# A down projection in two phases, with its weight sums made in DRAM: an encoder layer on one Trainium2 core

## The chip, the cores and the metric

The kernel runs on one core of a Trainium2 chip. TensorE (PE) multiplies, VectorE (DVE), ScalarE (ACT) and GpSimd (POOL) work on the elements, SyncE (SP) issues most of the transfers, and POOL issues some of its own. The metric is the device time of one execution in microseconds; less is better.

## The reference

One layer of a streaming encoder, for a prompt of 1024 frames and a sample of 32 frames, in float32. Both groups lie side by side as T = 1056 token columns.

```python
h = rms_norm(x); z = h @ w_in              # split into qa ka va | qb fb ib ob | ga gb
ya = sliding_window_attention(qa, ka, va)  # 16 query heads, 2 kv heads, sink logits, bias
yb = hgrn2(qb, fb, ib, ob)                 # gated recurrence, 8 heads
x = x + rms_norm((sig(ga) * (ya @ w_br_a) + sig(gb) * (yb @ w_br_b)) @ w_out)
a, u = split(rms_norm(x) @ w_up)           # two halves of 2816
a = causal_conv3(a)
x = x + rms_norm((gelu(a) * u) @ w_down)   # w_down is 2816 x 1024
y = x + (p @ w_ple) * sig(x @ w_ple_gate)
```

## The kernel before

Activations lie with features on the 128 partitions and tokens along the row. Every float32 factor is split into a rounded high part and a low part (ACT makes the high part by a cast, DVE the low part by a subtraction), and a product is three matmuls: high by high, high by low, low by high.

The stages run one after another: norm and attention (to about 330 us), the recurrence, branch mix and output projection, the up projection with the convolution (units of L2060 to L2140), the down projection (L2188 to L2270), and the gate of the last line of the reference.

The **up and down projections** use a block scheme with seven products instead of eight: the weight is cut in 2 x 2 blocks, the activations too, and sums of blocks are multiplied. For the weight of the down projection with blocks a11, a12, a21, a22, the seven left factors are: 0: a11, 1: a11+a21+a22, 2: a12, 3: a11+a21, 4: a21+a22, 5: a22, 6: a12 + factor 1. The right factors (sums of activation blocks) are written to DRAM by the up projection, in `s_d` and `a_d`, and loaded again as operands `dop`.

The down projection runs over three parts of the 2816 rows (`KP`, 3, 4 and 4 pairs of row blocks) and in each over four pairs of output column blocks: 12 units (`down_unit`) of seven products. A product is 2 token halves x 3 or 4 row groups x 3 matmuls of 264 columns, in all 1848 matmuls. In a unit:

- SP loads the four weight blocks (`wd`, L1757); POOL makes the block sums with four additions (L1780 to L1787, into `sa` and in place); ACT and DVE split each of the seven factors into `wt` (L1773, L1774). `prepare` runs this three products ahead.
- Three PSUM tiles X, Y, Z of the tag `st` (three buffers in all) take the products; each product's result is added up at once into up to three of the four output blocks `acc` and into a common term `S` (L2225 to L2231), by ACT in the first part and by DVE in the others.
- In the last unit of a part, operand i of the next part is loaded (L2045) as soon as product i has used the old one, and split some products later (L2050, L2051). For the first part that happens in the last unit of the up projection.

The last unit of all runs its two token halves one after the other, so that the norm of the first half (`x2_norm`) can be made beside the second half.

The instructions are not executed in the order of the code: a scheduler places each engine's instructions, and an instruction without anything to wait for can move far ahead of its place in the code. Within an engine the order that results is fixed, and each engine works through its own in order. That holds for the transfers too: one that POOL issues stands in POOL's order. The transfers of POOL carry eight completion semaphores in turn (DMASW0 to DMASW7), and each waits for the one that used its semaphore before: at most eight are under way.

In the attention, POOL has a small part: it copies the sink logits into the last column of each score tile (`sc`, L498), where ACT's exponential reads them (L505); PE then transposes the probabilities (L531). POOL also moves the sample's keys (`K`, L337), and issues adding transfers that make the low parts of some weights (`wl`, L183).

Of the kernel before, what the change touches and what calls it, by code (L numbers as in the profile page):

```python
# [59 lines left out]
def layer_kernel(  # L60
# [66 lines left out]
    s_d = {o: dp.tile([P, NF // 2, 2, H], F32, name=f"s_d{o}") for o in (1, 3, 4, 5)}  # L127
    pw_d = [dp.tile([P, 1024], F32, name=f"pw_d{i}") for i in range(11)]
# [946 lines left out]
    with right("bp") as bp:  # L1075
# [661 lines left out]
    KP = ((0, 3), (3, 4), (7, 4))  # L1737
    DU = [(pt, cp_) for pt in range(3) for cp_ in range(4)]
    NU = NF + len(DU)

    def groups(u):
        return 4 if u < NF else KP[DU[u - NF][0]][1]

    def unit_raw(u):
        t = []
        if u < NF:
            pool, tag, bufs = (wp, "wr", 2) if u % 2 == 0 else (fp, "wx", 2)
            for h in (0, DFF):
                t.append(pool.tile([P, KT, P], F32, tag=tag, name=nm("wu"), bufs=bufs))
                dma(t[-1][:], rows_cols(w_up, 0, h + u * P, P, KT)[0])  # L1750
        else:
            tag, bufs = ("wr", 2) if u % 2 else ("wb", 8)
            pt, cp_ = DU[u - NF]
            j0, n = KP[pt]
            for c in (2 * cp_, 2 * cp_ + 1):
                t.append(wp.tile([P, KT, P], F32, tag=tag, name=nm("wd"), bufs=bufs))
                dma(t[-1][:, :2 * n], rows_cols(w_down, 2 * j0 * P, c * P, P, 2 * n)[0])  # L1757
        raw_w[u] = t

    def unit_parts(u, s1, place, out):  # L1760

        f1, f2 = raw_w.pop(u)
        n = groups(u)
        if u < NF:
            a11, a12, a21, a22 = f1[:, 0:4, :], f1[:, 4:8, :], f2[:, 0:4, :], f2[:, 4:8, :]
        else:
            a11, a12, a21, a22 = (f[:, :2 * n].rearrange("p (j a) c -> p a j c", a=2)[:, a]
                                  for f in (f1, f2) for a in range(2))
            s1 = s1[:, :n]

        def parts(i, src):
            t = place(i)
            S.copy(t[:, 0, :n], src)  # L1773
            V.tensor_tensor(t[:, 1, :n], src, t[:, 0, :n].bitcast(F32), op=ALU.subtract)  # L1774
            out(i, t)
# [61 lines left out]
    def prepare(n):  # L1837

        while n_parts[0] < min(n + 1, 7 * NU):
# [7 lines left out]
            if i == 3 and u + 1 < NU:  # L1847
                unit_raw(u + 1)
            n_parts[0] += 1


# [168 lines left out]
    def act_sums(j):  # L2020

        (b11, b12), (b21, b22) = act_blocks(2 * j), act_blocks(2 * j + 1)
        sm = fp.tile([P, T + 2], F32, tag="a", name=nm("sm"), bufs=2)
# [29 lines left out]
    SPLIT_AT = {3: 0, 4: 1, 6: 2, 7: 3, 9: 4, 10: 5, 11: 6}  # L2053

    def split_step(pt, s):
        if s in SPLIT_AT:
            for p in range(2):
                with behind(S, V):
                    split_op(pt, p, SPLIT_AT[s])
# [3 lines left out]
    def up_unit(u):  # L2063
# [62 lines left out]
        for ps, steps in (((0,), first_), ((1,), early)) if u == 0 else (((0, 1), order),):  # L2126
            for n, (i, t, first, then) in enumerate(steps):
# [6 lines left out]
                if u == NF - 1:  # L2134
                    for p in range(2):
                        load_op(0, p, i)
                    split_step(0, n)
# [30 lines left out]
    for _ in act_sums(NF // 2 - 1):  # L2168
        pass
# [5 lines left out]

    def ep_q(name):
        return ep.tile([P, 2, H], F32, tag="q", name=nm(name), bufs=4)

    sqd = [ep_q("sqd") for _ in range(2)]
    acc_t = [ep.tile([P, 4, 2, H], F32, name=f"acc{i}") for i in range(3)]  # L2180
    acc_t = [acc_t[1], acc_t[2], acc_t[0]]
    S_ = page(lq, 3, [P, 4, 2, H], "S").bitcast(F32)

    def acc_of(cp_):
        if cp_ == len(acc_t):
            acc_t.append(page(lq, 2, [P, 4, 2, H], "acc3").bitcast(F32))
        return acc_t[cp_]

    def down_unit(u):

        pt, cp_ = DU[u - NF]
        ng = KP[pt][1]
        last = pt == 2
        X, Y, Z = (pf.tile([P, 2, 512], F32, tag="st", name=nm("st"), bufs=3) for _ in range(3))
        acc = acc_of(cp_)
        split_p = u == NU - 1

        def mults(i, t, first, ps):
            w = ready_w[7 * u + i]
            for p in ps:  # L2200
                o = t[:, p, 0:H]
                for k in range(ng):
                    wh, wl = w[:, 0, k, :], w[:, 1, k, :]
                    xh, xl = ops[p][i][:, 0, k, :], ops[p][i][:, 1, k, :]
                    E.matmul(o, wh, xh, start=first and k == 0, stop=False, skip_group_check=True)  # L2205
                    E.matmul(o, wh, xl, start=False, stop=False, skip_group_check=True)  # L2206
                    E.matmul(o, wl, xh, start=False, stop=k == ng - 1, skip_group_check=True)  # L2207

        def square(c, h, sl):
            src = acc[:, 2 * c + h, sl]  # L2210
            if cp_ == 0 and c == h:
                S.activation(sqd[h][:, sl], src, AF.Square)
            else:
                sq = ep_q("sq")
                S.activation(sq[:, sl], src, AF.Square)
                (V if split_p else G).tensor_tensor(sqd[h][:, sl], sqd[h][:, sl], sq[:, sl], op=ALU.add)

        def after(i, ps):
            sl = slice(ps[0], ps[-1] + 1)
            x, y, z_ = (t[:, sl, 0:H] for t in (X, Y, Z))  # L2220
            s = S_[:, cp_, sl]
            c11, c12, c21, c22 = (acc[:, b, sl] for b in range(4))

            def add(o, a, op=ALU.add):
                V.tensor_tensor(o, o, a, op=op)  # L2225

            if pt == 0:
                if i == 1:
                    S.mul(c12, y, -1.0)  # L2229
                elif i in (0, 2, 3, 5):  # L2230
                    S.copy({0: s, 2: c11, 3: c22, 5: c21}[i], {0: x, 2: x, 3: y, 5: y}[i])  # L2231
                elif i == 4:
                    add(c22, z_, ALU.subtract)
                else:
                    add(c12, z_)
                return
            if i == 0:
                add(s, x)
                if last:
                    add(c12, s)  # L2240
                    add(c22, s, ALU.subtract)
                    add(c21, s, ALU.subtract)
            elif i == 1:
                add(c12, y, ALU.subtract)
            elif i == 2:
                add(c11, x)
            elif i == 3:
                add(c22, y)
            elif i == 4:
                add(c22, z_, ALU.subtract)  # L2250
            elif i == 5:
                add(c21, y)
            else:
                add(c12, z_)
            if last and i in (2, 4, 5, 6):
                square(*{2: (0, 0), 4: (1, 1), 5: (1, 0), 6: (0, 1)}[i], sl)

        steps = ((0, X, True), (1, Y, True), (2, X, False), (3, Y, False), (4, Z, True), (5, Y, False),
                 (6, Z, False))
        for ps in ((0,), (1,)) if split_p else ((0, 1),):  # L2260
            for n, (i, t, first) in enumerate(steps):
                if ps[0] == 0:
                    prepare(7 * u + n + AHEAD)
                mults(i, t, first, ps)
                if cp_ == 3 and not last:
                    for p in range(2):
                        load_op(pt + 1, p, i)
                    split_step(pt + 1, n)
                if cp_ == 0:
                    split_step(pt, 7 + n)  # L2270
                after(i, ps)
                if split_p:
                    beside_last(ps[0], n)

    def conv_tails():
        for s, dst in ((0, o_pconv), (1, o_sconv)):
            b = tr_bank()
            E.transpose(b[:44, 0:P], tails[:, s].rearrange("p j f -> p (j f)"), ident[:])
            t = ep.tile([44, P], F32, tag="q", name=nm("tl"), bufs=4)
            S.copy(t[:], b[:44, 0:P])  # L2280
            dma(dst[0, 0].rearrange("j (f p) -> (j f) p", p=P), t[:])


    gw, graw, xh, xl, x1s = {}, {}, [None] * 4, [None] * 4, []

    def gate_raw(c):
        graw[c] = wp.tile([P, KT, P], F32, tag="wr", name=nm("wg"), bufs=2)
# [262 lines left out]
```

## Time and profile before

| | |
|---|---|
| three runs | 2001.23, 2003.19, 2005.37 us, median 2003.19 |
| the profiled execution | 2004.12 us, its span 2002.0 us, 38330 instructions |
| DMA in the span | 251.39 MB, 279229 packets, of them POOL's queue 32.73 MB in 10080 |
| POOL's waits for the `sa` buffer in the down projection (L1780, on PE) | 57.1 us in 5 waits |

How to read it: a window row has for each engine the busy time and the number of instructions, and at its end the granted clock of TensorE (1.00 is full speed), the mean busy share of the 16 DMA engines (it can read a little above 1) and the rate in GB/s. A timeline row has the start, the duration, and in brackets how long the engine sat idle before it and what ended that. PE is busy nearly everywhere, and so any time that PE stands still is added to the whole.

### The profile page before, as it was taken

To read this page: it belongs to the slowest core of one execution; us is meant where nothing else is said; L and a number is where in the kernel's file an instruction comes from. 1 tells how busy PE (TensorE), PEld (TensorE's weight loads), DVE (VectorE), ACT (ScalarE), POOL (GpSimd) and SP (SyncE) were. 2 spreads that over 40 slices of the span, in tenths; PEclk is the share of its full clock that TensorE was granted. 3 is DMA by queue.
4 is the path that set the end of the run, shared out by engine and by line. 5 is a ranking of instruction groups with operands and counts; after the bars stand their busy time and mean duration, and the time that the engine had idled before them with its cause. 6 is when DMAs were issued, how large, how long until landed. Compare 5 with 4: busy or idle time off the path is not lost. (4 is left out here: it accounts for less than half of the span.)

```text
span 2002.0 us, 38330 instructions
## 1 busy us (share of the span) xinstructions
PE 1951.9 (98%) x14715; PEld 1930.4 (96%) x14715; DVE 1470.4 (73%) x3160; ACT 997.7 (50%) x2175; POOL 338.3 (17%) x449
## 2 busy tenths in 40 slices
PE   8999999999999999999999999999999979999998
PEld 8999999999999999999999999999999979999998
DVE  6777776888878888553555888888888884767861
ACT  7667676666656666441235753333333344433432
POOL 2111110000000000012001232332323332224100
PEclk9999999999999999999999999999999989999999
DMA  8534432311121222486576753333233354461542
GB/s 269 150 89 111 132 98 76 124 41 54 54 79 54 58 58 74 149 260 203 167 222 203 264 171 102 104 108 110 95 104 100 109 178 130 139 186 51 150 112 85
DMA packets 279229, 251.39 MB, mean 126 GB/s; under 512 B 13381, under 2 KB 257224, under 8 KB 279045
## 3 DMA queue, kind: packets, MB, share of 16 engines
q1 hardware_dynamic: 268965, 216.20, 35.0%
q0 software_dynamic: 10080, 32.73, 5.4%
q8 instruction: 116, 1.90, 0.4%
q14 instruction: 68, 0.56, 0.1%
HBM read 163.74 MB, written 77.21 MB: 120 GB/s over the span
## 5 line engine op out<-in xcount | busy, mean ns | idle before, releaser
L2080 PE MATMUL st<-op,wt 128*128 128x264 f32 x1232 | 350.7, 285 | 8.0 <-DVE Sp L2093 4.6
L2082 PE MATMUL st<-op,wt 128*128 128x264 f32 x1232 | 350.4, 285 | 0.0
L2081 PE MATMUL st<-op,wt 128*128 128x264 f32 x1232 | 348.5, 283 | 0.0
L2080 PEld LDWEIGHTS st<-op,wt 128*128 128x128 f32 x1232 | 232.0, 188 | 11.6 <-DVE Sp L2093 6.1
L2081 PEld LDWEIGHTS st<-op,wt 128*128 128x128 f32 x1232 | 232.1, 188 | 0.0
L2082 PEld LDWEIGHTS st<-op,wt 128*128 128x128 f32 x1232 | 231.5, 188 | 0.0
L2205 PE MATMUL st<-dop,wt 128*128 128x264 f32 x616 | 177.5, 288 | 20.8 <-DVE acc L2225 10.2
L2206 PE MATMUL st<-dop,wt 128*128 128x264 f32 x616 | 176.4, 286 | 2.5 <-DVE dop L2051 2.5
L2207 PE MATMUL st<-dop,wt 128*128 128x264 f32 x616 | 176.6, 287 | 0.0
L199 PE MATMUL mm<-La,wh 128*128 128x384 f32 (+1 forms) x480 | 158.2, 330 | 0.0
L200 PE MATMUL mm<-Lb,wh 128*128 128x384 f32 (+1 forms) x480 | 155.4, 324 | 0.6 <-DVE Lb L769 0.6
L201 PE MATMUL mm<-La,wl 128*128 128x384 f32 (+1 forms) x480 | 154.9, 323 | 0.2 <-DVE wl L744 0.2
L1773 ACT CAST wt<-wu 128x512 fp32r<-128x512 f32 x126 | 77.0, 618 | 155.8 <-PE st L2082 65.2
L199 PE MATMUL mm<-Ra,wh 128*128 128x264 f32 x512 | 145.4, 284 | 0.0
L200 PE MATMUL mm<-Rb,wh 128*128 128x264 f32 x512 | 145.0, 283 | 0.0
L201 PE MATMUL mm<-Ra,wl 128*128 128x264 f32 x512 | 145.0, 283 | 0.0
L2205 PEld LDWEIGHTS st<-dop,wt 128*128 128x128 f32 x616 | 117.9, 191 | 23.2 <-ACT acc L2229 9.8
L2206 PEld LDWEIGHTS st<-dop,wt 128*128 128x128 f32 x616 | 117.9, 191 | 3.0 <-DVE dop L2051 3.0
L2207 PEld LDWEIGHTS st<-dop,wt 128*128 128x128 f32 x616 | 117.7, 191 | 0.0
L1774 DVE TENSOR_TENSOR wt<-wu,wt 128x512 fp32r<-128x512 f32 x126 | 92.6, 743 | 29.5 <-ACT wt L1773 29.5
L200 PEld LDWEIGHTS mm<-Rb,wh 128*128 128x128 f32 x512 | 96.5, 188 | 0.0
L199 PEld LDWEIGHTS mm<-Ra,wh 128*128 128x128 f32 x512 | 96.4, 188 | 0.0
(568 smaller groups left out, 6075.7 us busy)
## 6 DMA issues: line engine op xcount, KB each, us to landing
wu<-in_w_up_dram SPq DMA_DIRECT2D x42, 512.0 KB
wu<-in_w_in_dram SPq DMA_DIRECT2D x36, 512.0 KB
a_d<-Up SPq DMA_DIRECT2D x22, 528.0 KB
s_d<-sm SPq DMA_DIRECT2D x44, 264.0 KB
wr<-in_w_in_dram SPq DMA_DIRECT2D x21, 512.0 KB
dop<-s_d SPq DMA_DIRECT2D x16, 528.0 KB
wr<-in_w_out_dram SPq DMA_DIRECT2D x16, 512.0 KB
wd<-in_w_down_dram SPq DMA_DIRECT2D x16, 512.0 KB
```

What stands on the lines that cost most here:

```text
L199: E.matmul(ps, wh, a, start=first and n == 0, stop=False)
L200: E.matmul(ps, wh, b, start=False, stop=False)
L201: E.matmul(ps, wl, a, start=False, stop=last and n == len(ks) - 1)
L1773: S.copy(t[:, 0, :n], src)
L1774: V.tensor_tensor(t[:, 1, :n], src, t[:, 0, :n].bitcast(F32), op=ALU.subtract)
L2080: E.matmul(o, wh, xh, start=first and k == 0, stop=False, skip_group_check=True)
L2081: E.matmul(o, wh, xl, start=False, stop=False, skip_group_check=True)
L2082: E.matmul(o, wl, xh, start=False, stop=k == 3, skip_group_check=True)
L2205: E.matmul(o, wh, xh, start=first and k == 0, stop=False, skip_group_check=True)
L2206: E.matmul(o, wh, xl, start=False, stop=False, skip_group_check=True)
L2207: E.matmul(o, wl, xh, start=False, stop=k == ng - 1, skip_group_check=True)
```

## The change

It has four parts.

1. **Weight sums by transfers.** Four new arrays in DRAM, `w_d` for factors 1, 3, 4 and 6, take the sums for the whole down projection: 16 transfers copy a block of the weight (128 x 11 pieces of 512 bytes, 704 KB each), and 16 add to it with the transfers' own addition. Factor 1 needs factor 4 done, and 6 needs 1. POOL issues all 32; in the code they stand spread over the pieces of the recurrence. POOL's 48 additions of the down projection go.
2. **Two phases.** In each part, products 0 to 2 run for all four column pairs, and then products 3 to 6 for all four. The operands of the second phase are loaded and split during the first, and those of the next part's first phase during the second (`phase_step`).
3. **Fewer additions and banks.** Products 0 and 1 collect over the three parts in `S` and the new `T1`, and are brought into the output blocks once (`rest`). A unit takes two PSUM tiles, not three. Each weight factor is loaded by itself (`d_raw`, two to a tile) and split five products ahead.
4. **The end.** The last two column pairs run the first token half, then the second in the opposite order, with the norm, the gate's weights and the first pairs of the gate beside them. The last sums of the up projection run beside the first products of the down projection.

```diff
+    w_d = {o: dp.tile([P, 4, NF // 2, P], F32, name=f"w_d{o}") for o in (1, 3, 4, 6)}
+    dv = w_down[0].rearrange("(j a p) (c h n) -> p a h c j n", a=2, p=P, h=2, n=P)
...
+        w_sums = [(3, 0, 0, None), (4, 0, 1, None), (1, 0, 0, None), (6, 1, 0, None),
+                  (3, 0, 1, None), (4, 1, 1, None), (1, None, None, 4), (6, None, None, 1)]
+        for n, (o, a, h, other) in enumerate(w_sums):
+            for c in range(4):
+                def w_sum(o=o, src=w_d[other][:, c] if other else dv[:, a, h, c], c=c,
+                          op={"accum_op": ALU.add} if n > 3 else {}):
+                    gdma(w_d[o][:, c], src, **op)
+                at(8 + 5 * (4 * n + c), w_sum)
...
+    OPS = ((0, 1, 2), (3, 4, 5, 6))
+    D_ORDER = [(pt, c, i) for pt in range(3) for ph in OPS for c in range(4) for i in ph]
...
+    def d_raw():
+        k = len(raw_d)
+        t = wp.tile([P, KT, P], F32, tag="wr", name=nm("wd"), bufs=2)
+        raw_d.append(t)
+        for a in range(2):
+            pt, c, i = D_ORDER[2 * k + a]
+            j0, n = KP[pt]
+            z_ = slice(j0, j0 + n)
+            src = w_d[i][:, c, z_] if i in w_d else dv[:, i // 2 % 2 + i // 5, i // 5, c, z_]
+            dma(t[:, 4 * a:4 * a + n], src)
...
-                if u and u % 2 == 0 and n in (2, 5):
-                    if n == 2:
+                if u > 1 and n == 2 + u % 2:
+                    if u % 2 == 0:
                         sums_of.append(act_sums(u // 2 - 1))
...
+    def evacuate(pt, c, i, t, ps):
+        sl = slice(ps[0], ps[-1] + 1)
+        acc, x = acc_of(c), t[:, sl, 0:H]
+        o = {0: S_[:, c], 1: T1_[:, c], 2: acc[:, 0], 3: acc[:, 3], 4: acc[:, 3], 5: acc[:, 2],
+             6: acc[:, 1]}[i][:, sl]
+        if i == 4:
+            add(o, x, ALU.subtract)
+        elif pt == 0:
+            S.copy(o, x)
+        else:
+            add(o, x)
...
+    def rest(c):
+        acc = acc_t[c]
+        r = S_[:, c]
+        V.tensor_tensor(r, T1_[:, c], r, op=ALU.subtract)
+        add(acc[:, 1], r, ALU.subtract)
+        add(acc[:, 3], r)
+        add(acc[:, 2], r)
...
+        X, Y = st_bank(), st_bank()
+        banks = {0: (X, True), 1: (Y, True), 2: (X, False), 3: (X, True), 4: (Y, True), 5: (X, False),
+                 6: (Y, False)}
...
+    for seg in range(3):
+        for ph in range(2):
+            if seg == 2 and ph == 1:
+                break
+            for c in range(4):
+                def beside(n, c=c):
+                    phase_step(seg, ph, len(OPS[ph]) * c + n)
+                    if (seg, ph) == (0, 0) and n == 1 and c < 2:
+                        with behind(V):
+                            next(last_sums)
+                d_unit(seg, ph, c, beside=beside)
```

Two places of the scheduled order matter for what follows. The first is POOL's order in the first 60 us, in the attention. Before, the load of the sinks is followed by the sample's keys (`K` from `kh`) and the sink copies (`sc`):

```order
L697 DMA nsink<-in_attn_sinks_dram 128x16
L716 COPY tb_181<-tb 32x128
L599 MEMSET x_431 32x1024
L600 MEMSET x_431 64x1024
L411 MEMSET qa_1007 128x64
L337 DMA K_0_169<-kh_872 64x32 x2
L337 DMA K_1_170<-kh_872 64x32 x2
L913 MEMSET sc_794 128x256
L917 COPY nsink_796<-nsink 32x8 x2
L498 COPY sc_946<-nsink 128x2
```

With the change, the same stretch, from the second memset of `x` on (four copies stand ahead of it already; w_d_143 to w_d_146 are the arrays of factors 1, 3, 4 and 6):

```order
L602 MEMSET x_435 64x1024
L1441 DMA w_d_145<-in_w_down_dram 128x11x128 x4
L1441 DMA w_d_143<-in_w_down_dram 128x11x128 x4
L1441 DMA w_d_146<-in_w_down_dram 128x11x128 x4
L413 MEMSET qa_1011 128x64
L1441 DMA w_d_144<-in_w_down_dram 128x11x128 x3
L339 DMA K_0_173<-kh_876 64x32 x2
L339 DMA K_1_174<-kh_876 64x32 x2
L1441 DMA w_d_144<-in_w_down_dram 128x11x128
L915 MEMSET sc_798 128x256
L919 COPY nsink_800<-nsink 32x8 x2
```

The transfers did not stay in the recurrence where the code has them: all 16 copies and the four additions for factor 3 (the last two rows with w_d_144) now stand ahead of the first sink copy. The other 12 additions follow between the later sink copies of the first head pair and those of the second:

```order
L500 COPY sc_1367<-nsink 128x2
L1441 DMA w_d_143<-w_d_145 128x1408
L500 COPY sc_1429<-nsink 128x2
L1441 DMA w_d_143<-w_d_145 128x1408 x2
L500 COPY sc_1592<-nsink 128x2
L1441 DMA w_d_143<-w_d_145 128x1408
L1441 DMA w_d_146<-w_d_143 128x1408 x2
L500 COPY sc_1627<-nsink 128x2
L1441 DMA w_d_146<-w_d_143 128x1408 x2
L500 COPY sc_1669<-nsink 128x2
```

Before, no transfer stood among these sink copies; now each comes only after the transfers ahead of it have been issued.

The second place is ACT's order at the start of the down projection. Before, the evacuation of product 1 (`acc` at L2229) stands behind three weight casts whose sources POOL has summed:

```order
L1971 ACTIVATE a_19997<-a_19997 128x1058
L1773 CAST wt_20167<-wd_20036 128x384
L1773 CAST wt_20189<-wd_20036 128x384
L1773 CAST wt_20215<-wd_20038 128x384
L2229 ACTIVATE acc_20027<-st_20031 128x528
L2231 COPY acc_20027<-st_20030 128x528
```

With the change the casts (L1869) read what SP loaded, and the evacuations (L2232) stand among them:

```order
L1992 ACTIVATE a_20017<-a_20017 128x1058
L2232 COPY S_20039<-st_20130 128x528
L2071 CAST dop_20073<-dop_20073 128x792
L2232 COPY T_20035<-st_20041 128x528
L2232 COPY acc_20037<-st_20040 128x528
L1869 CAST wt_20222<-wd_20132 128x384
```

No row of POOL is left between the loads of a weight factor and its cast.

More of the change, by code (lines that the diff above doesn't have):

```diff
@@ L2051, in split_op, with split_ops @@
         V.tensor_tensor(lo, lo.bitcast(F32), hi.bitcast(F32), op=ALU.subtract)
[L2053 to L2059, printed above, removed]
+    def split_ops(pt, i, ps=(0, 1)):
+        for p in ps:
+            with behind(S, V):
+                split_op(pt, p, i)
     sums_of = []
@@ L2186, in acc_of @@
             acc_t.append(page(lq, 2, [P, 4, 2, H], "acc3").bitcast(F32))
-        return acc_t[cp_]
-    def down_unit(u):
-        pt, cp_ = DU[u - NF]
-        ng = KP[pt][1]
[L2193 to L2212, printed above, removed]
-            else:
[L2214 to L2281, printed above, removed]
+        return acc_t[c]
+    def st_bank():
+        return pf.tile([P, 2, 512], F32, tag="st", name=nm("st"), bufs=3)
+    D_AHEAD = 5
@@ new lines, in conv_tails, with y_small @@
+    def conv_tails():
+        for s, dst in ((0, o_pconv), (1, o_sconv)):
+            b = tr_bank()
+            with behind(E):
+                E.transpose(b[:44, 0:P], tails[:, s].rearrange("p j f -> p (j f)"), ident[:])
+            t = y_small(s)[:44, 0:P]
+            S.copy(t, b[:44, 0:P])
+            dma(dst[0, 0].rearrange("j (f p) -> (j f) p", p=P), t)
+    def y_small(n):
+        return xs_page[0][:, 3].rearrange("p a c -> p (a c)")[:, 256 * (n % 2):256 * (n % 2) + 256]
+    gate_raw(0)
@@ new lines, in layer_kernel, with beside @@
+    gate_raw(1)
+    for c in range(2):
+        def beside(n, c=c):
+            if n == 0:
+                with behind(V):
+                    rest(c)
+            if n == 1:
+                square(c, 0)
+            if n == 2:
+                with behind(S, V):
+                    gate_parts(2 * c)
+            if n == 3 and c == 0:
+                with behind(S, V):
+                    gate_parts(1)
+        d_unit(2, 1, c, beside=beside)
+    def beside(n):
+        if n == 0:
+            with behind(V):
+                rest(2)
+        if n == 1:
+            square(2, 0)
+        if n == 2:
+            with behind(V):
+                rest(3)
+        if n == 3:
+            square(3, 0)
+            xs_page.append(ep.tile([P, 4, 2, H], F32, tag="T1", name="xs"))
+            for c in range(3):
+                x1_load(0, c)
```

333 lines of the change are left out of this document (189 added, 144 removed).

## The prediction

> **What bounds the kernel now.** The page comes first, then windows of 100 us.
>
> ```profile
> span 2002.0 us, 38330 instructions
> PE 1951.9 (98%) x14715; PEld 1930.4 (96%) x14715; DVE 1470.4 (73%) x3160; ACT 997.7 (50%) x2175; POOL 338.3 (17%) x449
> ...
> 0.00:100.00 100.00, 93.72 (x594) 87.29 (x594) 67.30 (x182) 67.08 (x152) 17.97 (x53) 1.00 0.68 210
> ...
> 1500.00:1600.00 100.00, 99.34 (x820) 99.13 (x819) 82.83 (x127) 33.39 (x47) 32.85 (x25) 1.00 0.32 105
> 1600.00:1700.00 100.00, 86.38 (x685) 84.71 (x684) 64.89 (x93) 45.18 (x75) 29.46 (x20) 0.93 0.49 152
> ```
>
> PE is the bound, and time is lost where PE stands still. At its full pace (1500 to 1600 us, 820 matmuls of 264 columns) one matmul takes 100 / 820 = 0.122 us. In the down projection the pace drops, and the granted clock with it. Its matmuls are found by the operand `dop`, and PE's waits there by the list of waits from 1615 to 1890 us:
>
> ```profile
> L2205 PE MATMUL st<-dop,wt x616: 278/282/587, 1625.9 to 1882.0; 128*128 128x264 f32 x154
> L2207 PE MATMUL st<-dop,wt x616: 278/283/425, 1626.1 to 1882.3; 128*128 128x264 f32 x154
> ...
> PE st L2205 <- DVE acc L2225: 10.2, 7, 2.7
> PE st L2205 <- ACT acc L2229: 9.5, 1, 9.5
> PE st L2206 <- DVE dop L2051: 2.5, 2, 2.1
> ```
>
> The three lines of a product (the second has as many) have 616 matmuls each, 1848 in all, from 1625.9 to 1882.4 us, which is the last start and one matmul: 256.5 us. At full pace they need 1848 x 0.122 = 225.4 us. So **31 us are lost in the down projection**, 22 of them in the waits shown, the rest mostly in the clock, which falls after a stand. The longest wait is explained by the timeline of POOL and of ACT and by a window:
>
> ```profile
> 1643.38 3.71 POOL L1782 TENSOR_TENSOR wd<-wd,sa 128x384 f32<-128x384 f32 x1 [6.20 <-DVE wt L1774]
> ...
> 1647.12 1.34 ACT L1773 CAST wt<-wd 128x384 fp32r<-128x384 f32 x3 [6.75 <-POOL wd L1782]
> ...
> 1635.00:1650.00 15.00, 3.40 (x21) 2.82 (x20) 13.57 (x17) 6.48 (x12) 6.97 (x4) 0.63 0.19 73
> ```
>
> ACT stood for 6.75 us before a cast whose source POOL was still summing, the evacuation of PSUM stood behind that cast, and PE did 21 matmuls in 15 us at a clock of 0.63.
>
> **What the change takes away.** POOL's sums go, so the wait of 9.5 us has no cause left. Two PSUM tiles per unit out of three let the next unit start while the last result is still being evacuated, which takes the cause of the 10.2 us. Operands are loaded and split a whole phase ahead, which takes the 2.5 us; with the stands goes the low clock. The 1848 matmuls stay. What is late next is DVE: in the 15 us above it was busy for 13.57, and the convolution's tail, the last sums and the operand splits of the start are all still there. I leave 5 of the 31 us lost and count **-26 us**; the bounds are 10 (DVE holds PE nearly as before) and 31. SP's smaller weight loads (factors in place of blocks) I cost at nothing: DMA has a share of 0.49 in the window from 1600 to 1700. The moved sums of the up projection and the rewritten end also cost nothing here; PE has the same products there, and small errors are inside these bounds.
>
> **What it adds, and where.** The 32 transfers were moved by the scheduler into POOL's first 100 us. There POOL is in order, and has work on which PE depends:
>
> ```profile
> 8.00 0.52 POOL L666 DMA_DIRECT2D tb<-in_rel_bias_table_dram  x1 [1.31 <-DMA gvrows<-in_g_post_mix_dram]
> ...
> 59.59 0.68 POOL L498 COPY sc<-nsink 128x2 f32<-128x2 f32 x5
> ...
> 64.42 0.41 ACT L505 ACTIVATE sc<-sc,st 128x129 f32<-128x129 f32 x1 [0.64 <-DVE st L500]
> ...
> 66.08 0.38 PE L531 MATMUL tr<-ident,sc 128*128 128x128 f32 x2
> ...
> 92.26 0.19 POOL L498 COPY sc<-nsink 128x2 f32<-128x2 f32 x1 [6.50 <-PE tr L531]
> ```
>
> The first row shows the rule of eight: the tenth transfer of POOL waited 1.31 us for the second, whose semaphore it uses. The others show the chain: POOL copies the sinks, ACT takes the exponential at 64.4 us, and PE transposes at 66.1 us. PE runs in order, so a sink copy later than about 64 us stops PE.
>
> By the order of the change, the sample's keys and then the first sink copy stand behind the 16 copies and four additions; by the eight semaphores, 16 copies and three additions must have landed before it can run. What do they cost? No row of before shows a transfer from DRAM to DRAM. The nearest are a load of weights in pieces of 512 bytes (1318 to 1319 us), an adding transfer alone on the engines (232 to 234 us), and the fastest stretch of all:
>
> ```profile
> 16.00:18.00 2.00, 1.85 (x12) 1.51 (x11) 2.00 (x4) 2.00 (x5) 0.00 (x0) 1.00 1.04 397
> 232.00:233.00 1.00, 1.00 (x7) 1.00 (x7) 0.94 (x3) 0.97 (x5) 0.38 (x1) 1.00 1.01 197
> ...
> 1318.00:1319.00 1.00, 1.00 (x11) 1.00 (x10) 1.00 (x2) 0.00 (x0) 1.00 (x1) 1.00 0.97 283
> ```
>
> One transfer has 128 x 11 x 512 bytes = 0.721 MB. A copy at 283 / 0.97 = 292 GB/s takes 2.5 us of all 16 DMA engines; it could take 1.8 us (at 397 GB/s) or twice 2.5 if the second end in DRAM costs as much as the first. An addition at 197 GB/s takes 3.6 us; its bounds are 1.8 and 1.5 x 3.6 = 5.4 us (two reads and a write in DRAM, where the row has none). I take 2.5 and 3.6, since those rows have the same pieces and the same operation. The engines are not free then:
>
> ```profile
> 10.00:20.00 10.00, 9.04 (x52) 7.38 (x52) 9.17 (x16) 7.24 (x16) 1.26 (x3) 1.00 1.06 372
> 20.00:30.00 10.00, 9.97 (x62) 9.48 (x61) 6.76 (x15) 9.05 (x19) 1.51 (x3) 1.00 0.70 209
> 30.00:40.00 10.00, 9.26 (x58) 8.55 (x57) 6.64 (x13) 6.90 (x14) 0.00 (x0) 1.00 0.86 274
> 40.00:50.00 10.00, 9.63 (x65) 9.13 (x64) 6.39 (x18) 7.06 (x14) 0.00 (x0) 1.00 0.65 220
> 50.00:60.00 10.00, 9.59 (x70) 8.75 (x70) 7.41 (x26) 5.43 (x14) 3.10 (x11) 1.00 0.69 193
> 60.00:70.00 10.00, 9.63 (x62) 9.02 (x62) 8.50 (x29) 6.65 (x21) 3.18 (x12) 1.00 0.52 134
> ```
>
> From 10 to 64 us SP's own transfers fill 10.6 + 7.0 + 8.6 + 6.5 + 6.9 + 2.1 = 41.7 us of engine time. With 16 x 2.5 + 3 x 3.6 = 50.8 us more, the engines are through at 10 + 41.7 + 50.8 = 102.5 us, and the first sink copy comes then instead of by 64.4: **+38 us**. Up to the sink copy that stood at 92.26 us, nine more additions must land: 9 x 3.6 = 32.4 us, and SP's share of 0.52 (the last row) over 28 us is some 14 us, 46.4 us in place of 28: **+18 us**. These additions are a chain of three (factor 4, then 1, then 6), and a step can't be issued before the one ahead has landed, while sink copies that wait for PE stand between. For engines that run dry between steps I add 10 us, an estimate: two turns of about 5 us, the median from issue to landing of `wl` in the list of transfers:
>
> ```profile
> wl<-wr POOLq DMA_DIRECT2D x11, 512.0 KB, 4.9
> ```
>
> PE has no slack to take this back, and the recurrence, where DMA has room, is not where the transfers stand:
>
> ```profile
> 100.00:200.00 100.00, 100.00 (x703) 99.46 (x701) 77.06 (x247) 73.69 (x198) 17.43 (x53) 1.00 0.37 100
> ...
> 400.00:500.00 100.00, 100.00 (x675) 99.40 (x674) 84.54 (x234) 64.56 (x171) 3.28 (x12) 1.00 0.16 48
> ```
>
> From 100 us on PE has no idle time, and at 400 us DMA has a share of 0.16.
>
> **Sum**, against the profiled execution's 2004.1 us: 2004.1 - 26 + 38 + 18 + 10 = 2044; that execution is 0.9 us above the median of the runs, so 2043.
>
> A section of the Trainium skill speaks to the copies' price: "DMA: Bandwidth & Descriptors", "Latency and other measured facts", has copies between two arrays in HBM at 207 to 214 GB/s. By that a copy would take 3.4 us in place of 2.5, and the sum would be some 14 us higher, 2057; no run here shows such a copy yet.
>
> **Rivals.**
>
> *The transfers run at the peak.* If each takes 1.8 us, the first sink copy comes at 10 + 41.7 + 19 x 1.8 = 86 us, +22; the nine additions and SP's 14 us then fit the 28 us nearly (+2) and the chain costs nothing. With all 31 us gained, the time is 2003 + 24 - 31 = 1996. It decides where a transfer takes under about 2 us. For it: 397 GB/s were moved in the stretch from 16 to 18 us. Against it: the adding transfer above, alone on the engines, moved 197. Chance 0.24; the times around it lie on both sides of the bound of 0.2% (4 us, about what a measurement of this kernel can tell from no change): faster 0.16, same 0.08. The same page of the Trainium skill, "Anatomy of one DMA", gives 2 us plus bytes at 436 GB/s, so 1.65 us of moving per transfer, by which the loss would be about 19 us and the time about 1991; the row at 197 GB/s speaks against it for additions.
>
> *Both ends in DRAM cost.* At 5 us a copy and 5.4 us an addition, the first part is 10 + 41.7 + 96 = 148 us, +84; the second 9 x 5.4 + 14 - 28 = +35; with the chain's 10: 2003 - 26 + 129 = 2106. For it: the copies write and read the same memory in pieces of 512 bytes. Chance 0.15.
>
> *The down projection keeps its stands.* Then the change doesn't do what it says there; DVE's 13.57 of 15 us speak for it, POOL's part in the longest wait against. It gains 10, and the time is 2059. Chance 0.06.
>
> **How the numbers follow.** The forecast, 2043, has 0.55, with times from 2015 to 2080. Slower by over 0.2%: 0.55 + 0.15 + 0.06 = 0.76; same 0.08; faster 0.16. The range cuts the peak rival near its middle (0.12 left out below 1994) and the DRAM rival near its middle (0.08 left out above 2107).
>
> **What would show it.** Right: PE waits of tens of us between 60 and 130 us, put down to POOL or to the score tiles, POOL waiting for DMA before `K`, a down projection of about 230 us with the clock at 1.00. Wrong: sink copies at their old times although the transfers stand ahead of them (then the transfers are much faster than any row here); a down projection that still has a clock of 0.6 somewhere; or a new wait later, say on the weight factors that SP loads.

## The result, and the profile after

| | median us (lowest to highest) | ratio to before, 95% interval |
|---|---|---|
| before, four runs | 2002.53 (2001.23 to 2005.37) | |
| changed kernel, four runs | 2034.62 (2032.78 to 2036.66) | 1.0159 [1.0141, 1.0176] |

The changed kernel is **slower by 1.6%**. The forecast was 2043, with a range from 1994 to 2107. Its profiled execution took 2033.22 us. The head of its page, and windows of it:

```profile
span 2031.4 us, 38387 instructions
PE 1951.6 (96%) x14715; PEld 1930.4 (95%) x14715; DVE 1433.0 (71%) x3170; ACT 997.8 (49%) x2181; POOL 300.7 (15%) x423
...
0.00:100.00 100.00, 59.88 (x310) 53.24 (x311) 38.42 (x94) 39.69 (x76) 33.33 (x45) 0.80 1.00 287
100.00:200.00 100.00, 75.10 (x489) 72.12 (x487) 52.37 (x156) 47.14 (x128) 26.90 (x54) 0.90 0.88 173
1500.00:1600.00 100.00, 100.00 (x828) 100.00 (x827) 78.49 (x128) 33.81 (x49) 37.11 (x26) 1.00 0.31 101
...
1700.00:1800.00 100.00, 100.00 (x829) 100.00 (x828) 62.62 (x87) 54.13 (x85) 0.00 (x0) 1.00 0.68 219
```

PE is busy for as long as before (1951.6 against 1951.9 us), in a span 29.4 us longer. Before, PE had 93.72 and 100.00 us of work in the first two windows; now it has 59.88 and 75.10, and the clock is down to 0.80 and 0.90. Later windows are better than before: 828 matmuls in 100 us of the up projection where there were 820, and 829 from 1700 to 1800 us, in the down projection, where there were 737 before:

```profile
1700.00:1800.00 100.00, 92.91 (x737) 92.15 (x736) 73.86 (x84) 39.41 (x54) 28.01 (x18) 0.97 0.53 163
```

The changed kernel's down projection by its operand, and PE's waits from 1600 to 1920 us:

```profile
L2217 PE MATMUL st<-dop,wt x616: 279/282/391, 1687.5 to 1917.8; 128*128 128x264 f32 x154
L2219 PE MATMUL st<-dop,wt x616: 278/283/293, 1687.7 to 1918.1; 128*128 128x264 f32 x154
...
PE st L2217 <- DVE acc L2222: 1.9, 2, 1.6
PE st L2217 <- ACT S L2232: 1.3, 1, 1.3
```

The waits of 10.2, 9.5 and 2.5 us are gone, and the 1848 matmuls take from 1687.5 to 1918.2 us, 230.7 us instead of 256.5. The stages are bounded by the first matmuls of the up projection in both traces, and of the changed kernel's down projection above:

```profile
L2080 PE MATMUL st<-op,wt x1232: 279/282/422, 1161.5 to 1625.5; 128*128 128x264 f32 x176
```

```profile
L2098 PE MATMUL st<-op,wt x1232: 279/282/390, 1231.9 to 1687.1; 128*128 128x264 f32 x176
```

| stage | before us | after us | difference | forecast |
|---|---|---|---|---|
| all before the up projection | 1161.5 | 1231.9 | +70.4 | +66 |
| up projection | 464.4 | 455.6 | -8.8 | 0 |
| down projection | 256.5 | 230.7 | -25.8 | -26 |
| the rest | 119.6 | 113.2 | -6.4 | 0 |

The sum is +29.4, the difference of the spans. The whole of the +70.4 is lost by 400 us: the first exponential of a 128x129 score tile moved from 64.42 to 107.88 us (+43.5), and the last score matmul of the attention from 328.5 to 398.9 us (+70.4).

**What PE waited for.** The prediction had POOL's order hold up the sink copies, and so PE. The first stand (a stretch in which PE stands still) has another cause. PE's longest waits from 0 to 200 us, then POOL's and ACT's timelines, all of the changed kernel but the first row of POOL's, which is from before:

```profile
PE tr L533 <- DVE sc L510: 22.6, 3, 19.5
PE tr L302 <- ACT xc L775: 14.4, 1, 14.4
PE tr L644 <- ACT xc L775: 13.8, 1, 13.8
```

```profile
56.78 2.06 POOL L337 DMA_DIRECT2D K<-kh  x4 [35.17 <-ACT kh L222]
...
99.54 2.19 POOL L339 DMA_DIRECT2D K<-kh  x4 [45.89 <-ACT kh L224]
...
107.66 0.67 POOL L500 COPY sc<-nsink 128x2 f32<-128x2 f32 x5
```

```profile
46.53 0.48 ACT L775 COPY xc<-tr 128x384 f32<-128x384 f32 x1 [17.63 <-DMA xt_d<-xc]
63.94 0.48 ACT L775 COPY xc<-tr 128x384 f32<-128x384 f32 x1 [15.06 <-DMA xt_d<-xc]
...
153.72 1.04 ACT L180 CAST wh<-wr 128x1024 fp32r<-128x1024 f32 x1 [22.09 <-DMA wr<-in_w_in_dram]
```

PE waited for ACT's `xc`, not for a sink copy. POOL had issued its transfers and stood idle for 45.89 us until ACT had made the keys. It had waited so before, too, for 35.17 us: in both kernels the first sink copy stands behind the keys, and the prediction left that out. ACT stood twice, 17.63 and 15.06 us, for a buffer `xc` whose store to DRAM by SP had not landed. So the late one is SP. SP's timeline shows it as long issue rows (the duration of a row is what SP spent on issuing it), before and after:

```profile
18.29 1.65 SPq L774 DMA_DIRECT2D xt_d<-xc  x1
...
27.47 2.48 SPq L337 DMA_DIRECT2D K<-kh  x4
...
34.19 0.44 SPq L574 DMA_DIRECT2D h_d<-La  x1
```

```profile
22.95 14.69 SPq L776 DMA_DIRECT2D xt_d<-xc  x1
...
47.95 16.44 SPq L339 DMA_DIRECT2D K<-kh  x4
...
70.73 0.42 SPq L576 DMA_DIRECT2D h_d<-La  x1
...
130.62 19.54 SPq L294 DMA_DIRECT2D ta_d<-gt  x1
```

Four issues that took 2.48 us take 16.44, one store 14.69 instead of 1.65, and the first `h_d` is issued 36.5 us later. The list of DMA queues says why; first before, from 15 to 70 us, then after, in the same stretch (q1 is SP's queue, q0 POOL's; packets, MB, share of the 16 engines):

```profile
q1 hardware_dynamic: 11500, 12.02, 70.4%
q0 software_dynamic: 256, 0.07, 0.9%
```

```profile
q0 software_dynamic: 5335, 12.68, 82.4%
q1 hardware_dynamic: 4446, 4.28, 23.9%
```

SP moved 12.02 MB in these 55 us before, and 4.28 MB after, since POOL's 12.68 MB ran on the same engines. The Trainium skill, "DMA: Bandwidth & Descriptors", section "Queues, rings and completion order", says that each DMA engine takes turns between its queues packet by packet. The trace agrees, almost to the packet, where the engines are full. From 20 to 55 us, under POOL's copies:

```profile
q0 software_dynamic: 2381, 8.95, 83.4%
q1 hardware_dynamic: 2380, 1.89, 16.6%
```

A turn is not worth the same to both: a packet of POOL holds 8.95 MB / 2381 = 3.8 KB here, one of SP 0.8 KB, so POOL has 4.7 times the bytes.

In the second stand, near 140 us, PE waits for the score tile (19.5 us for `sc`, by DVE). DVE stood behind ACT, and ACT, in the last row of its timeline above, for 22.09 us for a weight `wr` that SP loads. SP's issue of `ta_d` in those microseconds took 19.54 us. From 140 to 160 us after, under POOL's additions from one new array to another:

```profile
q0 software_dynamic: 774, 3.89, 95.2%
q1 hardware_dynamic: 775, 0.40, 9.7%
```

Again the packets are equal, and POOL's of 5.0 KB against SP's of 0.5 KB leave SP 0.40 MB in 20 us. In other stretches the counts differ: from 60 to 70 us, when POOL's additions read the weight, POOL had 2290 packets of 0.7 KB and SP 719. Whether SP had fewer to send there, no run tells.

### The profile page after: what moved, and what is told of

Same layout as the page of the kernel before. It is cut to its first block, busy times and chain, and to the rows that moved or that the text cites. A ratio compares the mean times of both kernels' runs of the same rounds, so it can differ in the third digit from the quotient of the medians.

```text
span 2031.4 us, 38387 instructions
## 1 busy us (share of the span) xinstructions
PE 1951.6 (96%) x14715; PEld 1930.4 (95%) x14715; DVE 1433.0 (71%) x3170; ACT 997.8 (49%) x2181; POOL 300.7 (15%) x423
## 3 DMA queue, kind: packets, MB, share of 16 engines
q0 software_dynamic: 25696, 55.80, 10.7%
## 5 line engine op out<-in xcount | busy, mean ns | idle before, releaser
L2217 PE MATMUL st<-dop,wt 128*128 128x264 f32 x616 | 174.8, 284 | 3.3 <-DVE acc L2222 1.9
L2219 PE MATMUL st<-dop,wt 128*128 128x264 f32 x616 | 174.3, 283 | 0.0
L2218 PE MATMUL st<-dop,wt 128*128 128x264 f32 x616 | 174.0, 282 | 0.0
L2217 PEld LDWEIGHTS st<-dop,wt 128*128 128x128 f32 x616 | 115.7, 188 | 4.4 <-ACT wg L2336 1.8
L1763 DVE TENSOR_TENSOR wt<-wu,wt 128x512 fp32r<-128x512 f32 x126 | 86.4, 694 | 46.7 <-ACT wt L1762 46.7
L2218 PEld LDWEIGHTS st<-dop,wt 128*128 128x128 f32 x616 | 115.7, 188 | 0.0
L2219 PEld LDWEIGHTS st<-dop,wt 128*128 128x128 f32 x616 | 115.4, 188 | 0.0
L180 ACT CAST wh<-wr 128x1024 fp32r<-128x1024 f32 x51 | 53.4, 1048 | 97.5 <-PE mm L202 54.1
## 6 DMA issues: line engine op xcount, KB each, us to landing
w_d<-in_w_down_dram POOLq DMA_DIRECT2D x24, 704.0 KB, 21.3
```

What stands on the lines that cost most here:

```text
L180: S.copy(hi[:], raw[:])
L1763: V.tensor_tensor(t[:, 1], src, t[:, 0].bitcast(F32), op=ALU.subtract)
L2217: E.matmul(o, wh, xh_, start=first and k == 0, stop=False, skip_group_check=True)
L2218: E.matmul(o, wh, xl_, start=False, stop=False, skip_group_check=True)
L2219: E.matmul(o, wl, xh_, start=False, stop=k == ng - 1, skip_group_check=True)
```

## The experiments

Times are medians. Ratios are to runs of the kernel before on the same chip, whose median was 2002.84 us for the first four, 2003.13 for the next four and 2001.66 for the last two.

### The weight sums alone

The kernel before, with the transfers of the change (`w_d`, `dv` and `w_sums` as above) and nothing else; their results are not used:

```diff
+        for n, (o, a, h, other) in enumerate(w_sums):
+            for c in range(4):
...
+                    gdma(w_d[o][:, c], src, **op)
+                at(8 + 5 * (4 * n + c), w_sum)
```

> The kernel before, with the 32 transfers added as the change has them and their results not used; the down projection is the old one. Theory (the transfers in the first 160 us cost the 70 us by which the attention ends later in the changed kernel, whatever comes behind): about 2002 + 70 = 2072 us, attention scores ending near 399 us. Rival (part of the 70 us comes from other things that the change moved): clearly less, 2040 or below.

Measured: 2077.01 (2070.82 to 2077.92), ratio 1.0365 [1.0348, 1.0383], near the theory's 2072. The transfers cost 74 us by the medians. Its profiled execution, the lowest of its runs, has a span of 2069.0 us, 67 us more than before, and the same first stand as the changed kernel: ACT's waits for `xt_d` are 35.2 us in it, 36.3 in the changed kernel. With the 38.6 us that the rest of the change brings by the spans (next but one), 2002.0 + 67.0 - 38.6 = 2030.4, near the changed kernel's 2031.4. By the medians the sum is 2002.84 + 74.17 - 37.26 = 2039.75, 5 us above the changed kernel's 2034.62: the parts add up within that.

### One eleventh of the bytes

```diff
-                    gdma(w_d[o][:, c], src, **op)
+                    gdma(w_d[o][:, c, 0:1], src[:, 0:1], **op)
```

> As the run before, but each of the 32 transfers moves only the first of its 11 groups, 64 KB in place of 704 KB; the results are not used. They still stand ahead of the sample's keys and of the sink copies on POOL and still carry the eight semaphores in turn. Theory A (the engine time of the bytes costs, by crowding out SP's transfers and by the additions that must land): a loss of under 8 us, so 2003 to 2010 us. Theory B (the place in POOL's order costs, since each transfer waits for a landing of some 4 to 5 us: 32 x 4.5 / 8 for the semaphores and two chains more): 20 to 40 us of loss, so 2022 to 2042 us.

Measured: 2003.34, ratio 1.0004 [0.9994, 1.0014]. As many transfers, as many semaphores, and no loss: bytes are what costs. The places are not quite the same as in the changed kernel: with small transfers the scheduler set all 32 ahead of the first sink copy, on POOL a worse place. That copy ran at 60.37 us (before 59.59).

### The transfers held back

The changed kernel, where each transfer may no longer be moved ahead on POOL:

```diff
-                    gdma(w_d[o][:, c], src, **op)
+                    with behind(G):
+                        gdma(w_d[o][:, c], src, **op)
```

> The changed kernel, with each of the 32 transfers kept behind the POOL instruction that stands ahead of it in the code, so that they run in the recurrence. Theory (their early place is the whole loss, and DMA has room in the recurrence, with a share of 0.16 to 0.3): 2034.6 - 70 = 1964 us, within 5. Rival (POOL's waits for them then delay the recurrence's own POOL work, which loads the sample's states): 1975 to 2000 us. In the trace, the copies show what a transfer from DRAM to DRAM costs when it is nearly alone: 2.5 us of all engines by the prediction, 3.6 for an addition.

Measured: **1965.58** (1963.34 to 1967.28), ratio 0.9815 [0.9800, 0.9829], faster than both kernels. The page, and its row on `w_d`:

```profile
span 1963.4 us, 38382 instructions
...
w_d<-in_w_down_dram POOLq DMA_DIRECT2D x24, 704.0 KB, 10.7
```

The transfers are now issued from 332 to 724 us, in the recurrence; those of this row land 10.7 us after issue, not 21.3 (the same row of the changed kernel's page). No byte is saved; the attention's last score matmul is at 329.0 us (before 328.5), and the up projection begins at 1162.0 us (before 1161.5). So the transfers cost next to nothing there. The 38.6 us of the spans lie behind: the down projection begins at 1619.7 us, 6.2 earlier than before, takes 230.5, 26.0 less, and the rest 113.2, 6.4 less.

The prices can be read here nearly without SP's transfers. From 333 to 345 us the copies moved 2.85 MB in 0.838 x 12 = 10.1 us of all engines, 2.5 us for 0.721 MB; from 633 to 640 us additions from one new array to another 1.36 MB in 0.952 x 7 = 6.7 us, 3.5 us each. These are the prices of the prediction, 2.5 and 3.6.

### Copies early, additions held back

```diff
+                    with behind(*((G,) if op else ())):
+                        gdma(w_d[o][:, c], src, **op)
```

> The changed kernel, with the 16 copies at their early place and only the 16 additions kept in the recurrence. Theory A (SP's transfers are crowded out by the copies in the first 60 us): of the 48 us by which the first sink copy was late most stays, less some 10 us for the additions that were in flight there, and the 22 us behind it go: 1964 + 35 to 40 = 2000 us, and ACT waits for the stores of the transposed x between 30 and 65 us as in the changed kernel. Theory B (the waits for chained additions on POOL are the loss): 1964 to 1975 us.

Measured: 1999.49, ratio 0.9982 [0.9972, 0.9991], the time of theory A, with 34.2 us of waits of ACT for `xt_d`. Against the version with all held back, the 16 copies cost 33.9 us; against the changed kernel, the 16 additions cost 35.1. The first 128x129 exponential comes at 98.95 us, 34.5 later than before. POOL's queue from 15 to 70 us:

```profile
q0 software_dynamic: 3070, 11.53, 65.3%
```

These are the copies alone: 11.53 MB (16 of 0.721) in 0.653 x 55 = 35.9 us of all engines, 2.2 us a copy, beside SP's transfers.

### Five elevenths of the bytes

As with one eleventh, with `0:5` in place of `0:1`.

> The kernel before with the 32 transfers added at the same places and their results unused, each with 5 of its 11 groups of 128 columns. Theory A, engine time that first uses up what the engines have free (54 - 41.7 = 12.3 us up to the first sink copy): 10 + 41.7 + 50.8 x 5/11 = 74.8 us, +10; the additions 32.4 x 5/11 + 14 - 28 = +1; for chains that run dry 0 to 6; time 2014 to 2020. Rival L, a loss in proportion to the bytes: 74 x 5/11 = 34 us, time 2037. Rival T, that only full queues of SP cost, so that it is still free: 2003 to 2006.

Measured: 2036.53, ratio 1.0167 [1.0151, 1.0182]. The time is that of the rival of proportion, 17 to 23 us above the range of theory A. POOL's timeline shows what that expectation had wrong:

```profile
78.49 0.81 POOL L1441 DMA_DIRECT2D w_d<-w_d  x1 [1.34 <-DMA w_d<-w_d]
...
90.63 2.14 POOL L339 DMA_DIRECT2D K<-kh  x4 [11.13 <-ACT kh L224]
...
93.52 0.67 POOL L500 COPY sc<-nsink 128x2 f32<-128x2 f32 x5
```

The last of the 32 transfers is issued at 78.49 us, ahead of the first sink copy: here too the scheduler had set smaller transfers earlier. Counted in their real places, 10 + 41.7 + (16 x 2.5 + 16 x 3.6) x 5/11 = 96.1 us, and the sink copy ran at 93.52. The same sum for one eleventh gives 60.6 us, in time, and it ran at 60.37. So a sum of engine time gives both copies' times, and proportion does not: by it one eleventh would cost 6.7 us, and it cost 0.5. This reading was made after the run.

### Sink copies on DVE

The changed kernel, in which no exponential waits for POOL any more:

```diff
-            G.tensor_copy(sc8[:m_, 160:161], nsink8[:m_, i:i + 1])
+            V.tensor_copy(sc8[:m_, 160:161], nsink8[:m_, i:i + 1])
...
-            G.tensor_copy(sc[:m_, :, e_], nsink[:m_, 2 * i:2 * i + 2])
+            V.tensor_copy(sc[:m_, :, e_], nsink[:m_, 2 * i:2 * i + 2])
```

> The changed kernel with the sink copies (128x2 each) on DVE in place of POOL, so that no exponential waits for POOL's chain of additions any more; the 32 transfers stay on POOL, ahead of its casts and memsets for the second head pair, with all their bytes, and all is computed. Theory C (the second part of the loss is POOL's order: the sink copy stands behind an addition that waits for the one before it): the loss that the additions bring, 34 us between this case's e4_additions_held and the changed kernel, goes, and the time is 1999 to 2008. Theory A (the bytes hold back SP's transfers there as in the first part, wherever the sink copies stand): 2028 to 2036, and PE's stand near 140 us is put down to an operand that SP or POOL moves. In between, both have a share.

Measured: 2038.17 (2033.07 to 2039.86), ratio 1.0179 [1.0159, 1.0199]. Theory C falls; the time lies 2 us above the range of theory A. The loss of the additions stays, and PE's longest wait is longer than the changed kernel's 19.5 us. ACT's and PE's waits from 60 to 200 us, and SP's timeline:

```profile
ACT wh L180 <- DMA wr<-in_w_in_dram: 28.1, 1, 28.1
```

```profile
PE tr L533 <- DVE sc L510: 25.4, 1, 25.4
```

```profile
132.02 25.55 SPq L294 DMA_DIRECT2D ta_d<-gt  x1
```

ACT waits for SP's weight load, with the sink copies on POOL or not.

### The down projection without POOL's sums

The kernel before, with its sums in the down projection left out:

```diff
-        adder.tensor_tensor(s1, a21, a22, op=ALU.add)
...
+        sums = u < NF
+        if sums:
+            adder.tensor_tensor(s1, a21, a22, op=ALU.add)
...
```

> The kernel before, with the four block sums of each unit of the down projection left out (the up projection keeps its own), so POOL has nothing to do there; the factors are then plain blocks, and the output is not the reference's. It has the old load order, the old three banks and the old evacuations. Theory P: POOL's sums were the cause of the stand of 9.5 us and also slowed DVE (an operand split of DVE took 2.35 us beside a sum of POOL, 1.25 us otherwise, and the sum of 3.71 us takes 1.01 us elsewhere). Then the down projection falls from 256.5 to 236 to 242 us, no split takes over 1.3 us, and the time is 1984 to 1990. Rival B, that the banks and the late operands are the larger part: only the 9.5 us go, without the rest of the low clock, time 1992 to 1996. Rival D, that DVE holds PE at the start anyway: 1999 to 2003.

Measured: 1985.05 (1982.75 to 1986.98), ratio 0.9905 [0.9888, 0.9922]; the down projection takes from 1626.2 to 1866.3 us, 240.1 us. PE's waits there, and DVE's operand splits:

```profile
PE st L2208 <- ACT acc L2234: 4.6, 1, 4.6
...
PE st L2208 <- ACT acc L2232: 2.1, 1, 2.1
PE st L2208 <- DVE acc L2228: 1.5, 2, 1.0
PE st L2209 <- DVE dop L2054: 0.9, 2, 0.6
```

```profile
L2054 DVE TENSOR_TENSOR dop<-dop x42: 972/1248/1259, 1614.4 to 1797.9; 128x1056 fp32r<-128x1056 f32 x28, 128x792 fp32r<-128x792 f32 x14
```

Theory P holds for the time. 16.4 of the 25.8 us go with POOL's sums, and with them nearly all the 10.2 us for DVE's `acc`, though the three banks and the old evacuations are still there. Of the stand of 9.5 us for ACT's `acc`, 4.6 and 2.1 us are left although POOL does nothing, so its sums were not the only cause of that one. How they slow DVE is seen in the kernel before, on POOL, DVE and PE:

```profile
1698.24 2.19 POOL L1782 TENSOR_TENSOR wd<-wd,sa 128x512 f32<-128x512 f32 x1
```

```profile
1699.19 2.35 DVE L2051 TENSOR_TENSOR dop<-dop 128x1056 fp32r<-128x1056 f32 x1
...
1703.26 0.70 DVE L2225 TENSOR_TENSOR acc<-acc,st 128x528 f32<-128x528 f32 x1
```

```profile
1704.01 0.59 PE L2205 MATMUL st<-dop,wt 128*128 128x264 f32 x1 [2.73 <-DVE acc L2225]
```

A split that takes 1.25 us took 2.35 beside a sum of POOL; two more splits and then the evacuation stood behind it on DVE, and PE for 2.73 us behind that. The Trainium skill, "SBUF — State Buffer", section "SBUF: two separate sides", has an exclusive lock on ports that DVE and POOL share, held for a whole instruction. The traces agree: with nothing on POOL the longest split is 1.26 us.

### The sums on DVE

```diff
-        adder = V if u < 1 else G
+        adder = V if u < 1 or u >= NF else G
```

> The kernel before, with the block sums of the down projection on DVE in place of POOL; all is computed. The 48 sums would take about 0.6 us each on DVE (a weight split of 128x512 takes 0.68), some 29 us of the 256.5, where DVE is busy for 73% to 82%. Theory P (POOL's sums and their crossing with DVE's splits are the cause): the stand of 9.5 us shrinks to under 4, no split takes 2.35 us, and the time is 1988 to 1997. Rival D (DVE is late at the start, with 13.57 of 15 us busy): a stand of the same size is now put down to DVE, and the time is 2001 to 2015.

Measured: 1990.13, ratio 0.9934 [0.9921, 0.9946]. The time is theory P's, and the longest split is again 1.26 us; the stand at the start fell less than expected, to 6.5 us and not under 4 (one wait for ACT's `acc`). Moving 48 additions to the busier engine made the kernel 13 us faster, with everything computed.

### The spare bank

The changed kernel with its transfers held back, and:

```diff
-        X, Y = st_bank(), st_bank()
+        X, Y, _ = st_bank(), st_bank(), st_bank()
```

> The changed kernel with its transfers held back in the recurrence (e3_held_back, 1965.6 us), and a third PSUM tile taken by each unit of the down projection and not used, so that the next unit's first product can't go to a free one. Theory (the spare tile is what lets a unit start beside the last evacuation): each of the 24 units waits 1 to 2.5 us for the copy or addition that empties its tile (0.70 us and its signals), 24 to 60 us in all, time 1989 to 2025. Rival (the scheduler puts another product between, or the banks don't matter because the evacuations are short now): 1964 to 1972.

Measured: 1966.25 (1964.87 to 1969.66), ratio 0.9827 [0.9812, 0.9841], against 0.9815 with the spare bank: the rival's. The 24 waits did not come; which of the rival's two reasons holds was not looked up. The profiled execution, the slowest of the four, has one wait of 4.1 us for `S` where there was one of 1.0, and a down projection of 236.2 us in place of 230.5, so a few microseconds for the spare bank are not excluded.

### The old sums of the up projection

The held-back version, with the activation sums where they stood:

```diff
-                if u > 1 and n == 2 + u % 2:
-                    if u % 2 == 0:
+                if u and u % 2 == 0 and n in (2, 5):
+                    if n == 2:
```

> The changed kernel with its transfers held back in the recurrence (e3_held_back, 1965.6 us), and the activation sums of the up projection again where they were before (both halves of a sum in one unit, at its products 2 and 5). Theory: moving them is what took the up projection from 464.4 to 455.6 us (waits of PE for DVE's Sp, 4.6 us in 7, are gone), so the time is 1972 to 1976, the up projection about 464 us and the waits are back. Rival: the gain comes from the loads and splits ahead that the new prepare makes, then 1964 to 1968.

Measured: 1973.51 (1971.24 to 1975.24), ratio 0.9851 [0.9836, 0.9865], 7.9 us more than without the edit. PE's waits there:

```profile
PE st L2099 <- DVE Sp L2112: 4.6, 7, 0.7
```

It is the wait that the kernel before had, 4.6 us in 7, and the changed kernel not. The up projection takes 462.7 us, against 457.7 without the edit (464.4 before, 455.6 in the changed kernel; 464 was expected). So the theory holds in direction: one half of a sum in each unit, rather than both in every other unit, gave the up projection 5.0 us by this pair of traces, and 7.9 us by the medians of the whole time; the rest of its 8.8 us was not tried apart.

## Why the prediction was right, and where not

- **The sign and the size** came out: +70.4 early against +66, and -25.8 in the down projection against -26. Early, the price of a copy and of a chained addition was right and the way to PE wrong, so that the single terms came near is in part luck.
- **First sink copy, +38.** It was set at 102.5 us and ran at 107.66; PE lost 43.5 us there. That the loss is engine time was right (a kernel with one eleventh of the bytes loses nothing). The way from the transfers to PE was wrong: not POOL's order, but SP's stores, which got few bytes in each turn, while POOL stood idle for 45.89 us, before `K` as foretold, but for ACT's keys and not for DMA. Nor are the engines full up to the end, as the sum has it: with the copies alone it would give 10 + 41.7 + 35.9 - 64.4 = +23, and they gave +34.5. That SP's late stores then wait for PE and ACT would explain the difference; it was not measured apart.
- **Additions, +18 and +10.** +27 was lost behind the first stand (70.4 - 43.5). An addition from one new array to another took 3.5 us (0.952 x 20 us for 3.89 MB in the rows above, and the same with the transfers held back), as put down; one that reads the weight has no price of its own here, since the shares of both queues add up to more than 100% in those stretches (99.3% and 30.6% from 60 to 70 us). The mechanism put down, a sink copy behind a chain on POOL, failed: with the sink copies on DVE the loss stayed. The PE wait was named rightly (score tiles) and its cause wrongly.
- **Down projection, -26.** The sum is right. Of the reasons, POOL's sums bore more than was put on them (16.4 us, with most of the 10.2 us of waits that the prediction put down to the banks), but they were not the whole cause of the stand of 9.5 us, of which 6.7 us stayed without them. The banks bore no part that the medians show once the rest was changed. The other 9.4 us go with the load order, the evacuations and the phases together; these were not tried apart. DVE was not late next.
- **Up projection and end at nothing.** This is the step that failed in size: -8.8 and -6.4 us. The up projection had waits of 4.6 us in all, 7 of them, in the trace of before that the prediction left out. Of the end, 4.9 us are the gap between the last product and the gate (1882.4 to 1887.3 us before, none after); no run took the end apart.
- **Against 2043.** The differences from the terms are 4.4 - 8.8 + 0.2 - 6.4 = -10.6 us, and the profiled 2044 becomes 2033, which is what that execution took.
- **The rivals.** A copy ran near the forecast, at 2.5 us nearly alone and 2.2 beside SP's transfers, neither at the peak (1.8) nor at 5 us. The Trainium skill's page "DMA: Bandwidth & Descriptors" would have 3.4 us a copy by its section "Latency and other measured facts" and 1.65 by "Anatomy of one DMA"; the copies here lie between the two.

## What to carry to other kernels

Before a transfer is called hidden, look up where the scheduler has put it and what share the DMA engines have in that stretch: the same bytes cost 69 us at a share near 1, and next to nothing in a stretch that had been at 0.16 to 0.34. The engine in front of which PE stands need not be the one that issued the new transfers; follow each wait back to the first engine that waits for a landing, and compare the packets and the bytes of the queues. A sum moved off POOL can be worth more than its own time, where DVE works beside it.

## What was not expected of the hardware

- POOL's transfers take most of the engines from SP's: 12.68 MB to 4.28 MB in 55 us. Packet for packet the two queues are even (774 to 775 from 140 to 160 us), but POOL's packets were up to ten times as large. SP shows that as issue rows of 14.69 to 25.55 us, where their counterparts before took 0.34 to 2.48.
- A stand of PE costs more than its length. Behind the one at 140 us the granted clock (the third number from the end) is 0.50 while PE begins again, and 0.89 in the window after:

```profile
140.00:150.00 10.00, 0.00 (x0) 0.00 (x0) 0.00 (x0) 0.00 (x0) 2.62 (x4) 0.58 1.05 214
150.00:160.00 10.00, 3.36 (x15) 3.32 (x16) 3.14 (x8) 3.60 (x9) 1.81 (x3) 0.50 1.05 216
160.00:170.00 10.00, 7.46 (x43) 7.16 (x42) 2.05 (x6) 2.32 (x5) 0.00 (x0) 0.89 0.95 226
```

  Matmuls of 128x288 started 0.24 us apart from 158.42 to 161.06 us, and 0.13 us apart from 135.43 to 136.62 us, before the stand.
- Copies from DRAM to DRAM ran at 2.85 MB / 10.1 us = 283 GB/s nearly alone, additions from one new array to another at 3.89 MB / 19.0 us = 204 GB/s.
